# New homes for the split features and the contexts' matrices, input matrices on GpSimd's queue, and context rows that are turned without a trip to DRAM

## The chip, the cores and the metric

One of the eight cores of a Trainium2 chip runs the whole program. The metric is the device time of one execution in microseconds (us); a kernel's time is the median of several runs. A profile is one execution recorded by the chip's profiler, with instruction times counted from the start of its span.

## The reference

Two layers work on 512 latent tokens and 256 context tokens of width 1024, in float32. Each layer has a token mixer and a gated ConvFFN; layer 0 mixes by attention, layer 1 by a two-directional complex-diagonal state-space scan (S5). Each part is wrapped in RMSNorms with shift, scale and gate rows that come from conditioning vectors. Cut to what the change touches:

```
def conv_ffn(h, w_up, conv_w, conv_b, w_down):
    a = conv3(h @ w_up) + conv_b
    val, gate = split(a, 2)
    return (silu(gate) * val) @ w_down                       # D_FF = 2816

# end of layer 0, for latents and for contexts
x = x + m[5] * rms_norm(conv_ffn(h, ...), g_post_ffn[0])
# start of layer 1
h = modulate(rms_norm(x, g_pre_mix[1]), m[0], m[1])
# layer 1's mixer, for each of 2 directions
hc = s5_scan(u_c, lb, bb, None)          # contexts; u_c: 64 groups of 16 channels
hl = s5_scan(u_l, lb, bb, hc[end])       # latents start from the contexts' last state
y += s5_readout(hl, c)
o = (gelu(y + d*u) @ w_glu_a) * sigmoid(gelu(y + d*u) @ w_glu_b)
```

Contexts are needed in layer 1 only for the state in which they end.

## The kernel before

**Matmuls in three passes.** Float32 products are made of `fp32r` parts. Each weight block is split into a high and a low part, `whl` (ACT at L109, DVE at L110), and so are the features, `hs` (ACT at L942, DVE at L943). One product is then the three matmuls of L159, L160 and L161.

**The down projection of layer 0** (`ffn_down`, called twice from `ffn0`) goes over 22 blocks of 128 features. The first call makes three token tiles, the two of the contexts and the first of the latents; the second makes the latents' tiles 1 to 3. In each block, three tiles times two halves of the width times three passes are 18 matmuls of 128x512, named `dn`. The first three and the last four blocks are taken together, tile by tile (`together`), the others block by block. The call's `pool` (`self.hsp`) holds the split features `hs`, four slots in the first call and three in the second.

**The ends.** When a tile's product is complete, `done` calls `begin` and `end`. They multiply by the gate row (L741), take the statistics (ACT L740, and a row of tiny DVE instructions at L742 and L171 to L175), add the residual (L746), take statistics again (ACT L362) and modulate for layer 1 (L1035, L1036). Three gate, scale and shift rows, `rows`, are loaded broadcast to all partitions (L1010). The modulated tile `po` goes out by DMA: a context's to DRAM, `xnd` (L1038), a latent's into the SBUF tile `xc`, by blocks of 8 tokens (L1043). With the first call, the two contexts' and first latent tile's ends come between the two `ffn_down`; with the second call they are the last thing before the mixer.

**The contexts' part of layer 1** (`ssm_contexts`) is a generator. It loads `xcc` from `xnd` (L1571), reorders it (ACT L1425), transposes it on TensorE (`pu`, L1430) into `uc`, multiplies by the input matrices `Pt` (`pi`, L1494; eight groups of 512 KB pairs), turns the results back (`pb`, L1480; copied to `Bc` at L1485) and adds up states on DVE in two halves (`ssm_sums`, L1519 to L1522; `ssm_carry`, L1549 to L1552). `ffn_down` pulls steps of this generator between its blocks by `jobs=(24, 4, 15, jobs)` (24 steps spread over blocks 4 to 14), and its `before` pulls the rest ahead of the last four blocks.

**The latents' part** (`ssm`) begins with the loads of `lam` (L1555) and of further matrices, reorders `xc` into `xq` (L1425, on ACT and DVE), and transposes it (`pu`, L1430). `ssm_ahead` (L1396) makes a tile and a load for each matrix ahead of its use (L1411): `Pd` are the input matrices, `Qd` the output matrices. All of these loads go through SP's queue.

**What sets the order.** A tile scheduler orders each engine's queue from the order in which the program emits its instructions and from modelled costs. SBUF pools are stacks on a left and a right side; a tile placed on memory that another pool held waits for the last readers of what was there. In the kernel before, the second call's `hs` pool is made after `rowp` and lies on memory that the ends between the calls read.

Of the kernel before, what the change touches and what calls it, by code (L numbers as in the profile page):

```python
# [20 lines left out]
P = 128  # L21
# [13 lines left out]
G = 64  # L35
# [16 lines left out]
def dap(ap, off, dims):  # L52
    return bass.AP(tensor=ap.tensor, offset=ap.offset + off, ap=[list(d) for d in dims])
# [92 lines left out]
class Kernel:  # L146
# [831 lines left out]
    def ffn0(self):  # L978
# [28 lines left out]
        def rows_of(pool, lc):  # L1007
            t = pool.tile([P, 3, D], FT, name=f"rows{lc}")
            for i, (l, grp, m) in enumerate(((0, 2, 1), (1, 0, 0), (1, 0, 1))):
                nc.sync.dma_start(t[:, i], dap(self.mdram[l, grp], lc * 2048 + m * 1024, [[0, P], [1, D]]))  # L1010
            return [t[:, i] for i in range(3)]
# [7 lines left out]
        self.xnd = self.dram.tile([CTX, D], FT, name="xnd")  # L1019
# [7 lines left out]
        def end(wk, rows):  # L1027

            t, x = begun.pop(0)
            x, o = x()  # L1030
            if t >= NTC:
                nc.sync.dma_start(self.x2[t * P:(t + 1) * P, :], x)
            _, sh, gs = rows[int(t < NTC)]
            r = self.stats(x, wk.tile([P, D], BF, name="junk", tag="junk", bufs=1), "sx")
            v.tensor_tensor(o, x, gs, op=OP.mult)  # L1035
            self.mark = v.scalar_tensor_tensor(o, o, r, sh, op0=OP.mult, op1=OP.add).ins  # L1036
            if t < NTC:
                nc.sync.dma_start(self.xnd[t * P:(t + 1) * P, :], o)  # L1038
                return
            c, q = D // 2, nc.scalar if t == NT - 1 else nc.sync  # L1040
            for a in range(2):
                p0 = NCL * a + t - NTC
                q.dma_start(xc[p0:p0 + NCL - NT + NTC + 1:NT - NTC], o[:, a * c:(a + 1) * c])  # L1043
# [13 lines left out]
        rows = [rows_of(wk, i) for i in range(2)]  # L1057
# [38 lines left out]
        self.hsp.release()  # L1096
        rowp.release()
        si.release()
        self.hps[0].release()
# [296 lines left out]
    def ssm_ahead(self, loads, rooms, behind=None):  # L1396


        tiles = []
        rooms = [(pool, tag, bufs) for pool, tag, bufs in rooms for _ in range(bufs)]  # L1400
        for i in range(len(loads)):
            while len(tiles) < min(i + len(rooms), len(loads)):
# [8 lines left out]
                self.nc.sync.dma_start(t, src[:, gp:gp + n])  # L1411
                tiles.append(t)
            if i == 0:
                yield
# [144 lines left out]
    def ssm_contexts(self, si):  # L1559
# [7 lines left out]
        x = self.sb[1].tile([P, 2, 2048], FT, name="xcc", tag="B", bufs=1)  # L1567
        xcc = x[:, 0].rearrange("p (s c) -> p s c", s=TC)
        xq = x[:, 1].rearrange("p (g s c) -> p g s c", g=16, s=TC)
# [25 lines left out]
        for gp in self.ssm_inputs_turned(mats, lambda b: Bc[b // 2][:, b % 2], lambda g: uc[:, g % 16, g // 16], NCC, si):  # L1595
            if gp >= 12:
                next(first, None)
                next(first, None)
            yield
# [5 lines left out]
    def ssm(self):  # L1605
# [5 lines left out]
                              ((Rooms(None, Pt=[x[:, i] for x in hl for i in range(2)]), "Pt", 8), (sx, "Pt", 3)))  # L1611
# [12 lines left out]
        B = [x.tile([P, 2, NCL + 1, 2, 2, 8], FT, name="B", tag="B", bufs=1) for x in (self.sb[0], up)]  # L1624
        for i in range(2):
# [3 lines left out]
                            ((sp, "Qt", 8),), xq[0:1, 3, 7, 7, 15:16])  # L1629
# [279 lines left out]
```

## Time and profile before

| | |
|---|---|
| median of 3 runs | 1712.47 us (1712.05 to 1713.34) |
| the profiled execution | 1709.45 us |
| its span in the trace | 1707.7 us, 24431 instructions |
| TensorE busy (PE) | 1549.5 us, 91% |
| VectorE busy (DVE) | 1069.2 us, 63% |
| ScalarE busy (ACT) | 700.6 us, 41% |
| GpSimd busy (POOL) | 66.9 us, 4% |
| mean granted clock of TensorE | 0.958 of full speed |
| first `ffn_down`'s last matmul ends | 940.9 us |
| second `ffn_down`'s matmuls | 960.7 to 1072.9 us |
| the latents' first transpose | 1105.2 us |

Busy time is averaged over stages with different limits, so the shares say little by themselves; the stretch from 935 to 1110 us has to be read row by row. A row of the timeline gives start, duration, engine, line, operation and output from inputs; in brackets stands how long the engine was idle before it and what ended that wait. A queue's issues are marked with a "q" behind the engine's name.

### The profile page before, as it was taken

How to read it: one execution, taken by the hardware profiler on the slowest of the kernel's cores; microseconds unless marked ns; L12 is line 12 of the kernel's file. 1: busy time of each engine (PE TensorE's matmuls, PEld its weight loads, DVE VectorE, ACT ScalarE, POOL GpSimd, SP SyncE). 2: the span in 40 equal slices, each digit the busy share in tenths (PEclk: the TensorE clock that was granted, in tenths of full speed). 3: DMA queues.
4: the chain of work that ended last, by engine and by line, in shares of the span. 5: the costliest groups of instructions: out<-in, count | busy, mean ns of one | idle time of the engine just before them, and what ended most of it. 6: DMA issues, size and time to landing. Idle time of an engine off the chain costs nothing.

```text
span 1707.7 us, 24431 instructions
## 1 busy us (share of the span) xinstructions
PE 1549.5 (91%) x9300; PEld 1236.5 (72%) x9300; DVE 1069.2 (63%) x2185; ACT 700.6 (41%) x1379; POOL 66.9 (4%) x86
## 2 busy tenths in 40 slices
PE   5999789999999999989999599246999999999997
PEld 2775568888788887767888477234778887788886
DVE  4653687769777776777544636689535654545334
ACT  4465547756434333233343344241245443333322
POOL 0111230000000000000000000000011000000000
PEclk8999799999999999999999799677999999999999
DMA  9424450086445766686663665843544333432421
GB/s 311 133 74 144 170 186 26 30 271 226 144 142 159 204 165 194 141 239 145 221 247 139 191 232 171 266 152 93 155 134 133 94 106 116 126 110 100 159 74 50
DMA packets 223259, 263.44 MB, mean 154 GB/s; under 512 B 21038, under 2 KB 173526, under 8 KB 222502
## 3 DMA queue, kind: packets, MB, share of 16 engines
q1 hardware_dynamic: 222422, 261.28, 49.7%
q8 instruction: 73, 1.20, 0.3%
q10 hardware_dynamic: 336, 0.54, 0.1%
q14 instruction: 44, 0.36, 0.1%
q0 software_dynamic: 384, 0.07, 0.0%
HBM read 223.89 MB, written 35.85 MB: 152 GB/s over the span
## 4 chain that ended last, share of the span: by engine, by line
PE 79%; DVE 11%; DMA 4%; ACT 2%; SPq 1%; issue 1%; POOL 0%; DVEq 0%; ACTq 0%
PE up L159 11%; PE up L161 11%; PE up L160 11%; PE dn L159 6%; PE dn L160 6%; PE dn L161 6%; PE acc L159 2%; PE acc L161 2%; PE acc L160 2%; PE glu L161 2%; PE glu L159 2%; PE macc L301 2%; PE glu L160 2%; PE py L1703 1%; DMA wm<-in_w_mod 1%; PE wo L159 1%
## 5 line engine op out<-in xcount | busy, mean ns | idle before, releaser
L110 DVE TENSOR_TENSOR whl<-wraw,whl 128x1024 fp32r<-128x1024 f32 x206 | 250.8, 1223 | 170.4 <-ACT whl L109 168.7
L109 ACT ACTIVATE whl<-wraw 128x1024 fp32r<-128x1024 f32 x206 | 216.6, 1056 | 203.9 <-PE dn L161 100.3
L159 PE MATMUL up<-b,whl 128*128 128x256 f32 (+1 forms) x728 | 244.2, 339 | 5.1 <-ACT whl L109 4.5
L161 PE MATMUL up<-b,whl 128*128 128x256 f32 (+1 forms) x728 | 242.3, 334 | 0.2 <-DVE whl L110 0.2
L160 PE MATMUL up<-b,whl 128*128 128x256 f32 (+1 forms) x728 | 241.8, 334 | 0.1
L159 PE MATMUL dn<-whl,hs 128*128 128x512 f32 x440 | 173.1, 397 | 19.8 <-ACT hs L942 19.8
L160 PE MATMUL dn<-whl,hs 128*128 128x512 f32 x440 | 173.9, 397 | 0.0
L161 PE MATMUL dn<-whl,hs 128*128 128x512 f32 x440 | 171.9, 394 | 0.0
L159 PEld LDWEIGHTS up<-b,whl 128*128 128x128 f32 x728 | 136.7, 188 | 31.2 <-issue 9.6
L161 PEld LDWEIGHTS up<-b,whl 128*128 128x128 f32 x728 | 136.7, 188 | 17.8 <-issue 3.4
L160 PEld LDWEIGHTS up<-b,whl 128*128 128x128 f32 x728 | 137.3, 189 | 15.7 <-issue 1.8
L877 DVE SCALAR_TENSOR_TENSOR ga<-up,cw,ga 128x511 f32<-128x511 f32 (+1 forms) x132 | 87.0, 659 | 93.6 <-ACT ga L873 92.1
L160 PE MATMUL up<-c,whl 128*128 128x512 f32 (+1 forms) x384 | 142.3, 372 | 0.0
L159 PE MATMUL up<-c,whl 128*128 128x512 f32 (+1 forms) x384 | 141.7, 375 | 0.7 <-DVE c L352 0.7
L161 PE MATMUL up<-c,whl 128*128 128x512 f32 (+1 forms) x384 | 142.0, 372 | 0.0
L159 PEld LDWEIGHTS dn<-whl,hs 128*128 128x128 f32 x440 | 83.5, 190 | 40.8 <-ACT hs L942 20.3
L873 ACT ACTIVATE ga<-up,cw 128x512 f32<-128x512 f32 x66 | 46.6, 706 | 159.3 <-PE up L161 157.7
L877 DVE SCALAR_TENSOR_TENSOR h<-up,cw,h 128x511 f32<-128x511 f32 (+1 forms) x132 | 86.8, 658 | 34.8 <-ACT h L873 33.5
L160 PEld LDWEIGHTS dn<-whl,hs 128*128 128x128 f32 x440 | 83.4, 190 | 20.1 <-issue 2.5
L161 PEld LDWEIGHTS dn<-whl,hs 128*128 128x128 f32 x440 | 83.2, 189 | 18.2 <-issue 0.4
L159 PEld LDWEIGHTS up<-c,whl 128*128 128x128 f32 x384 | 71.9, 188 | 17.0 <-issue 4.1
L161 PEld LDWEIGHTS up<-c,whl 128*128 128x128 f32 x384 | 72.2, 188 | 13.4 <-issue 0.4
(354 smaller groups left out, 2833.5 us busy)
## 6 DMA issues: line engine op xcount, KB each, us to landing
wraw<-in_w_up SPq DMA_DIRECT2D x88, 512.0 KB
wraw<-in_w_mod SPq DMA_DIRECT2D x80, 512.0 KB
wraw<-in_w_down SPq DMA_DIRECT2D x66, 512.0 KB
Pt<-Pd SPq DMA_DIRECT2D x32, 512.0 KB
wraw<-in_w_o SPq DMA_DIRECT2D x24, 512.0 KB
Pt<-Qd SPq DMA_DIRECT2D x32, 384.0 KB
wm<-in_w_mod SPq DMA_DIRECT2D x16, 512.0 KB
Pd<-Pb SPq DMA_DIRECT2D x16, 512.0 KB
```

What stands on the lines that cost most here:

```text
L109: nc.scalar.activation(w[:, 0], r, AF.Copy)
L110: e.tensor_tensor(w[:, 1], r, w[:, 0], op=OP.subtract)
L159: nc.tensor.matmul(out, a[0], b[0], start=start, stop=False)
L160: nc.tensor.matmul(out, a[0], b[1], start=False, stop=False)
L161: nc.tensor.matmul(out, a[1], b[0], start=False, stop=stop)
L301: nc.tensor.matmul(acc[32 * q:32 * q + 32], self.cT[:, k, :], w[:, 256 * q:256 * q + 256], start=(k == 0), stop=(k == KD - 1))
L873: nc.scalar.activation(o, acc, AF.Identity, scale=c[:, 1:2], bias=c[:, 3:4])
L877: nc.vector.scalar_tensor_tensor(x, acc[:, a + s:b + s], c[:, tap:tap + 1], x, op0=OP.mult, op1=OP.add)
L1703: nc.tensor.matmul(y[hs, i], x, t[hs, 2 + 2 * ri + d], start=False, stop=ri + d == 2)
```

## The change

- The first call's ends are only recorded while it runs (`ended`). After the call its features' pool, a work pool and the contexts' features are released, the second call's pool `hsc` and a pool `si` for five `Pt` slots (three before) and `xcc` are made in their place, the first `Pd` loads are started, and then the recorded ends are emitted.
- The rows are tiles of their own. For the second call two of three lie in `hpx`, beside the residuals.
- A context's modulated tile goes straight into `xcc` in SBUF, by four DMAs; `xnd` and its loads go. `uc` lies beside the reordered tile.
- All 32 `Pd` loads are issued from GpSimd's queue. `Qd` stays on SP; its loads behind the first are held back to the first one's issue, which waits for the last reordering copy.
- In `ssm`, two tiles are made ahead of `lam` in their pool.

```diff
-            if t < NTC:
-                nc.sync.dma_start(self.xnd[t * P:(t + 1) * P, :], o)
-                return
-            c, q = D // 2, nc.scalar if t == NT - 1 else nc.sync
-            for a in range(2):
-                p0 = NCL * a + t - NTC
-                q.dma_start(xc[p0:p0 + NCL - NT + NTC + 1:NT - NTC], o[:, a * c:(a + 1) * c])
+            y, n, k, i, m = (xcc[0], NCC, 4, t, NTC) if t < NTC else (xc, NCL, 2, t - NTC, NT - NTC)
+            c, q = D // k, nc.scalar if t == NT - 1 else nc.sync
+            for a in range(k):
+                q.dma_start(y[n * a + i:n * a + i + n - m + 1:m], o[:, a * c:(a + 1) * c])
...
-        self.ffn_down(tiles, ((1, 0, CTX), (0, 0, P)), 4, done_of(wk, rows, tiles), ends=4,
+        ended, xcc = [], []
+        self.ffn_down(tiles, ((1, 0, CTX), (0, 0, P)), 4, lambda *x: ended.append(x), ends=4,
                       before=lambda: load(wk, tiles))
-        wk.release()
         self.hsp.release()
         self.wkD.release()
         self.hps[1].release()
+        self.hsp = self.pool("hsc")
+        si = self.pool("ssmi")
+        xcc.append(si.tile([P, TC, D // 4], FT, name="xcc"))
+        mats = self.ssm_ahead([(self.Pd, gp, 2) for gp in range(0, G // 2, 2)], ((si, "Pt", 5),), nc.gpsimd)
+        next(mats)
+        for x in ended:
+            done_of(wk, rows, tiles)(*x)
+        wk.release()
...
-        si = self.pool("ssmi")
         rowp = self.pool("rowp")
-        rows = [rows_of(rowp, 0), None]
-        self.hsp = self.pool("hsc")
+        rows = [None, None]
         self.W.fence = self.W.limit = self.glu0
-        jobs = self.ssm_contexts(si)
+        jobs = self.ssm_contexts(xcc[0], mats)
...
-            x = self.hps[0].tile([P, 3, D], FT, name="hpx", tag=f"h{LAT}0", bufs=1)
+            x = self.hps[0].tile([P, 5, D], FT, name="hpx", tag=f"h{LAT}0", bufs=1)
...
+            rows[0] = rows_of(0, [x[:, 3], x[:, 4], rowp.tile([P, D], FT, name="row")])
             self.mats = self.ssm_ahead([(self.Pd, gp, 2) for gp in range(0, 10, 2)],
-                                       ((self.wp, "raw", 5),))
+                                       ((self.wp, "raw", 5),), nc.gpsimd)
...
-    def ssm_ahead(self, loads, rooms, behind=None):
+    def ssm_ahead(self, loads, rooms, queue, behind=None):
...
-                self.nc.sync.dma_start(t, src[:, gp:gp + n])
+                x = queue.dma_start(t, src[:, gp:gp + n])
+                if behind is not None and not tiles:
+                    held.enter_context(self.tc.issue_after(x.ins))
...
-        mats = self.ssm_ahead([(self.Pd, gp, 2) for gp in range(0, G // 2, 2)], ((si, "Pt", 3),))
-        next(mats)
...
-        for a in range(4):
-            nc.sync.dma_start(xcc[NCC * a:NCC * a + NCC],
-                              dap(self.xnd, a * (D // 4), [[TC * D, NCC], [D, TC], [1, D // 4]]))
...
-        uc = si.tile([P, 16, 4, NCC], FT, name="uc")
...
-        for _ in self.ssm_turn(xcc, xq, uc, (nc.scalar,) * 4):
+        for _ in self.ssm_turn(xcc, xq, uc, (nc.scalar,) * 4, NTC):
...
         up = self.pool("ssmv")
+        B1 = up.tile([P, 2, NCL + 1, 2, 2, 8], FT, name="B", tag="B", bufs=1)
+        u = up.tile([P, G, NCL], FT, name="u")
         self.lam_tile(up.tile([P, 2048], FT, name="lam"))
         lamR, lamI = self.lam
-        u = up.tile([P, G, NCL], FT, name="u")
```

**ACT where the first call hands over to the second**, before. `hs` (L942) with 128x384 are the second call's split features, `whl` (L109) its split weights, and `junk` with `sp` or `sx` (L740, L362) the ends' statistics.

```order
L942 ACTIVATE hs<-h_4350 128x256
L942 ACTIVATE hs<-h_4348 128x128
L740 ACTIVATE junk,sp<-dn 128x512 x3
L109 ACTIVATE whl_9287<-wraw_8960 128x1024
...
L362 ACTIVATE junk,sx<-px 128x1024
L740 ACTIVATE junk,sp<-dn 128x512 x2
L362 ACTIVATE junk,sx<-px 128x1024 x2
L942 ACTIVATE hs<-h_4347 128x384 x3
```

And now:

```order
L942 ACTIVATE hs<-h_4350 128x256
L942 ACTIVATE hs<-h_4348 128x128
L942 ACTIVATE hs<-h_4347 128x384 x3
L740 ACTIVATE junk,sp<-dn 128x512 x3
L109 ACTIVATE whl_9292<-wraw_8963 128x1024
...
L362 ACTIVATE junk,sx<-px 128x1024
L740 ACTIVATE junk,sp<-dn 128x512 x2
L942 ACTIVATE hs<-h_4347 128x384
```

The second call's first three blocks of split features stand ahead of the ends' statistics instead of behind them; the fourth stands behind two of three tiles' statistics.

**TensorE at the contexts' last step**, now. `pb` (line 1480 before, 1485 now) turns the last results back; `dn` are the second call's matmuls.

```order
L161 MATMUL dn<-whl_10062,hs 128x512
L1485 MATMUL pb<-ident,pe 128x128 x4
L159 MATMUL dn<-whl_10065,hs 128x512
L160 MATMUL dn<-whl_10065,hs 128x512
```

Of the call's 396 `dn` matmuls, 378 stand ahead of this step and 18 behind; before, 341 stood ahead and 55 behind. The contexts' first `pu` stood behind 54 `dn` matmuls before, and stands behind 173 now.

**DVE at the second call's end**, before. `t` and `Bc` (L1519 to L1522) are the second half of the contexts' sums, `hpo<-dn` (L741) is the first instruction of a latent tile's end.

```order
L1521 TENSOR_TENSOR t<-Bc_9514,lamc 128x2x128
L1522 TENSOR_TENSOR Bc_9514<-Bc_9514,t 128x8x32
L1519 TENSOR_TENSOR t<-Bc_9514,lamc 128x128 x2
L741 TENSOR_TENSOR hpo<-dn,rows_9256 128x512
L1522 TENSOR_TENSOR Bc_9514<-Bc_9514,t 128x8x32
```

And now (the sums are at L1524 to L1527):

```order
L1526 TENSOR_TENSOR t<-Bc_9519,lamc 128x1024
L1527 TENSOR_TENSOR Bc_9519<-Bc_9519,t 128x32x32
L741 TENSOR_TENSOR hpo<-dn,hpx 128x512
L1524 TENSOR_TENSOR t<-Bc_9519,lamc 128x512 x2
L741 TENSOR_TENSOR hpo<-dn,hpx 128x512
L742 TENSOR_TENSOR sp<-sp 128x1
L1527 TENSOR_TENSOR Bc_9519<-Bc_9519,t 128x32x32
```

Two of the second half's instructions of sums stand ahead of the first end's instruction, where all but the last sum did before.

## Rows read from the trace of the kernel before

**Rows 1.** The page's chain that ended last: shares of the span by engine.

```profile
PE 79%; DVE 11%; DMA 4%; ACT 2%; SPq 1%; issue 1%; POOL 0%; DVEq 0%; ACTq 0%
```

**Rows 2.** Busy time by windows of 20 us (the columns are in its first row).

```profile
core 0: us, PE busy (x) PEld busy (x) DVE busy (x) ACT busy (x) POOL busy (x), PEclk, DMA share, GB/s
940.00:960.00 20.00, 0.88 (x4) 0.38 (x3) 19.68 (x55) 6.39 (x12) 0.00 (x0) 0.64 0.74 263
...
1080.00:1100.00 20.00, 0.00 (x0) 0.00 (x0) 14.27 (x45) 4.32 (x11) 0.00 (x0) 0.50 0.80 249
```

**Rows 3.** The timeline of PE around the handover from first to second call.

```profile
940.26 0.39 PE L160 MATMUL dn<-whl,hs 128*128 128x512 f32 x1
940.49 0.39 PE L161 MATMUL dn<-whl,hs 128*128 128x512 f32 x1
960.72 0.79 PE L159 MATMUL dn<-whl,hs 128*128 128x512 f32 x1 [19.84 <-ACT hs L942]
```

**Rows 4.** The timeline of ACT in the same stretch.

```profile
938.37 2.25 ACT L109 ACTIVATE whl<-wraw 128x1024 fp32r<-128x1024 f32 x2
940.92 1.06 ACT L109 ACTIVATE whl<-wraw 128x1024 fp32r<-128x1024 f32 x1 [0.30 <-PE dn L161]
...
960.14 1.35 ACT L942 ACTIVATE hs<-h 128x384 fp32r<-128x384 f32 x3 [4.24 <-DVE po L1036]
```

**Rows 5.** The timeline of PE, the latents' first transpose.

```profile
1105.17 2.15 PE L1430 MATMUL pu<-ident,xq 128*128 128x128 f32 x9 [32.29 <-DVE xq L1425]
```

**Rows 6.** The timeline of DVE before and behind the second gap.

```profile
1093.32 1.28 DVE L1036 SCALAR_TENSOR_TENSOR hpo<-hpo,rsx,rows 128x1024 f32<-128x1024 f32 x1
1104.60 1.43 DVE L1425 COPY xq<-xc 128x512 f32<-128x512 f32 x4 [9.99 <-DMA Pt<-Qd]
```

**Rows 7.** The timeline of ACT, contexts' last `Bc` and last store into `xc`.

```profile
1060.44 1.12 ACT L1485 ACTIVATE Bc<-pb 128x256 f32<-128x256 f32 x2 [2.83 <-PE pb L1480]
...
1094.64 1.26 ACTq L1043 DMA_DIRECT2D xc<-hpo  x2
```

**Rows 8.** The timeline of SP's queue, 930 to 1130 us.

```profile
960.14 1.24 SPq L1043 DMA_DIRECT2D xc<-po  x2
964.46 2.52 SPq L1571 DMA_DIRECT2D xcc<-xnd  x4
...
1030.43 48.17 SPq L1411 DMA_DIRECT2D Pt<-Pd  x21
...
1094.82 0.33 SPq L1555 DMA_DIRECT2D lam<-lamd  x1
1095.20 14.34 SPq L1411 DMA_DIRECT2D Pt<-Qd  x8
```

**Rows 9.** Windows of 2 us behind the handover (columns as in group 2).

```profile
964.00:966.00 2.00, 2.00 (x6) 1.52 (x5) 0.00 (x0) 0.00 (x0) 0.00 (x0) 0.50 0.06 15
966.00:968.00 2.00, 2.00 (x10) 1.64 (x9) 0.00 (x0) 0.00 (x0) 0.00 (x0) 0.97 1.05 237
```

**Rows 10.** The timeline of DVE, contexts' second half of sums.

```profile
1061.59 1.23 DVE L1521 TENSOR_TENSOR t<-Bc,lamc 128x1024 f32<-128x1024 f32 x1 [2.67 <-ACT Bc L1485]
...
1067.31 0.55 DVE L943 TENSOR_TENSOR hs<-h,hs 128x384 fp32r<-128x384 f32 x1
...
1071.82 0.69 DVE L741 TENSOR_TENSOR hpo<-dn,rows 128x512 f32<-128x512 f32 x1 [0.39 <-ACT junk L740]
1072.43 0.41 DVE L1522 TENSOR_TENSOR Bc<-Bc,t 128x256 f32<-128x256 f32 x1
```

**Rows 11.** GpSimd's instructions that issue DMAs: busy, mean ns of one, idle.

```profile
L313 POOL DMA_DIRECT2D md<-mbias x8 | 4.6, 570 | 715.1 <-DVE mbias L305 297.4 <-DVE mbias L309 178.8 <-DMA wraw<-in_w_mod 159.4
```

**Rows 12.** The view of the tile that those DMAs write.

```profile
DMA to landing us min/median/max: 2.0/3.8/6.0
```

**Rows 13.** PE's groups of lines, 960.7 to 1072.9 us.

```profile
L1494 PE MATMUL pi<-Pt,uc 128*32 128x256 f32 x128 | 12.0, 387 | 0.0
L1480 PE MATMUL pb<-ident,pe 128*128 128x128 f32 x32 | 4.9, 274 | 0.0
```

More of the change, by code (lines that the diff above doesn't have):

```diff
@@ L1005, in mods, with rows_of @@
                 yield from self.mods_ahead(ps, units, 2 - i)
[L1007 to L1011, printed above, removed]
+        def rows_of(lc, tiles):
+            for t, (l, grp, m) in zip(tiles, ((0, 2, 1), (1, 0, 0), (1, 0, 1))):
+                nc.sync.dma_start(t, dap(self.mdram[l, grp], lc * 2048 + m * 1024, [[0, P], [1, D]]))
+            return tiles
         self.ffn_up(0, ((self.act[0], LAT), (self.act[1], CTX)), "left", firsts,
@@ L1018, in ffn0 @@
         xc = sb0.tile([2 * NCL, TC, D // 2], FT, name="xc", tag="B", bufs=1)
-        self.xnd = self.dram.tile([CTX, D], FT, name="xnd")
         begun, loaded = [], {}
@@ L1056, in ffn0 @@
         wk = self.pool("wkE0", "right")
-        rows = [rows_of(wk, i) for i in range(2)]
+        rows = [rows_of(i, [wk.tile([P, D], FT, name=f"row{i}{j}") for j in range(3)]) for i in range(2)]
         tiles = (*range(NTC), NTC)
-        self.ffn_down(tiles, ((1, 0, CTX), (0, 0, P)), 4, done_of(wk, rows, tiles), ends=4,
+        ended, xcc = [], []
+        self.ffn_down(tiles, ((1, 0, CTX), (0, 0, P)), 4, lambda *x: ended.append(x), ends=4,
                       before=lambda: load(wk, tiles))
-        wk.release()
         self.hsp.release()
@@ L1095, in ffn0 @@
         self.ffn_down(tiles, ((0, P, LAT),), 3, done, jobs=(24, 4, 15, jobs), ends=4, before=before)
-        self.hsp.release()
         rowp.release()
         si.release()
+        self.hsp.release()
         self.hps[0].release()
@@ L1394, in lam_powers @@
         return lam
-    def ssm_ahead(self, loads, rooms, behind=None):
-        tiles = []
+    def ssm_ahead(self, loads, rooms, queue, behind=None):
+        tiles, held = [], ExitStack()
         rooms = [(pool, tag, bufs) for pool, tag, bufs in rooms for _ in range(bufs)]
@@ L1410, in ssm_ahead @@
                 t = t[:, :k].rearrange("p (a b n) -> p a b n", a=n, n=P)
-                self.nc.sync.dma_start(t, src[:, gp:gp + n])
+                x = queue.dma_start(t, src[:, gp:gp + n])
+                if behind is not None and not tiles:
+                    held.enter_context(self.tc.issue_after(x.ins))
                 tiles.append(t)
+            held.close()
             if i == 0:
@@ L1557, in lam_tile, with ssm_contexts @@
         self.lam = [lam[:, j] for j in range(2)]
-    def ssm_contexts(self, si):
+    def ssm_contexts(self, xcc, mats):
         nc, v, su = self.nc, self.nc.vector, self.su
         self.banks = (("aux", 2),)
-        mats = self.ssm_ahead([(self.Pd, gp, 2) for gp in range(0, G // 2, 2)], ((si, "Pt", 3),))
-        next(mats)
         lam = su.tile([P, 2, 4, 4, 2, 2, 8], FT, name="lamc")
         self.C0 = su.tile([P, 2, 2, 2, 2, 8], FT, name="C0")
-        x = self.sb[1].tile([P, 2, 2048], FT, name="xcc", tag="B", bufs=1)
-        xcc = x[:, 0].rearrange("p (s c) -> p s c", s=TC)
-        xq = x[:, 1].rearrange("p (g s c) -> p g s c", g=16, s=TC)
-        for a in range(4):
-            nc.sync.dma_start(xcc[NCC * a:NCC * a + NCC],
-                              dap(self.xnd, a * (D // 4), [[TC * D, NCC], [D, TC], [1, D // 4]]))
+        x = self.sb[1].tile([P, 2, 2048], FT, name="xqc", tag="B", bufs=1)
+        xq = x[:, 0].rearrange("p (g s c) -> p g s c", g=16, s=TC)
+        uc = x[:, 1].rearrange("p (g a j) -> p g a j", g=16, a=4)
         for i in range(4):
@@ L1594, in ssm_contexts @@
         first = half(0)
-        for gp in self.ssm_inputs_turned(mats, lambda b: Bc[b // 2][:, b % 2], lambda g: uc[:, g % 16, g // 16], NCC, si):
+        for gp in self.ssm_inputs_turned(mats, lambda b: Bc[b // 2][:, b % 2], lambda g: uc[:, g % 16, g // 16], NCC, sc):
             if gp >= 12:
@@ L1610, in ssm @@
         more = self.ssm_ahead([(self.Pd, gp, 2) for gp in range(10, G // 2, 2)],
-                              ((Rooms(None, Pt=[x[:, i] for x in hl for i in range(2)]), "Pt", 8), (sx, "Pt", 3)))
+                              ((Rooms(None, Pt=[x[:, i] for x in hl for i in range(2)]), "Pt", 8), (sx, "Pt", 3)), nc.gpsimd)
         next(more)
         up = self.pool("ssmv")
+        B1 = up.tile([P, 2, NCL + 1, 2, 2, 8], FT, name="B", tag="B", bufs=1)
+        u = up.tile([P, G, NCL], FT, name="u")
         self.lam_tile(up.tile([P, 2048], FT, name="lam"))
         lamR, lamI = self.lam
-        u = up.tile([P, G, NCL], FT, name="u")
         uv = u.rearrange("p (a g) j -> p g a j", a=2)
@@ L1623, in ssm @@
                 pass
-        B = [x.tile([P, 2, NCL + 1, 2, 2, 8], FT, name="B", tag="B", bufs=1) for x in (self.sb[0], up)]
+        B = [self.sb[0].tile([P, 2, NCL + 1, 2, 2, 8], FT, name="B", tag="B", bufs=1), B1]
         for i in range(2):
@@ L1628, in ssm @@
         qs = self.ssm_ahead([(self.Qd, gp, 1) for gp in range(G // 2)],
-                            ((sp, "Qt", 8),), xq[0:1, 3, 7, 7, 15:16])
+                            ((sp, "Qt", 8),), nc.sync, xq[0:1, 3, 7, 7, 15:16])
         next(qs)
```

## The prediction

> **What bounds the kernel now.** I read the page's chain first: three quarters and more of the span hang on TensorE [rows 1], so time is to be had where TensorE waits. The 20-us windows then show two holes, 940 to 960 us and 1080 to 1100 us, with 0.88 and 0.00 us of matmuls in 20; in both DVE is the busy engine, 19.68 and 14.27 us [rows 2].
>
> First hole: the first call's last matmul ends at 940.49 + 0.39 = 940.88, the second's first begins at 960.72 after 19.84 idle, ended by ACT's `hs` [rows 3]. On ACT that group of three splits had itself waited, 4.24 us, for DVE's L1036 [rows 4], the last instruction of the ends. The split reads features that were long there; what it waits for is memory that the ends still read. So the hole is a buffer's wait, while the weights for it were split at 938.37 to 941.98 [rows 4].
>
> Second hole: the last `dn` ends at T = 1105.17 - 32.29 = 1072.88 [rows 5]. DVE finishes the ends at 1093.32 + 1.28 = 1094.60, T + 21.7; then it is idle 9.99 us until its reordering copy at 1104.60 [rows 6]. The view blames a `Qd` load, but the copy reads `xc`, whose last stores ACT issued at 1094.64 [rows 7]. `lam` and eight `Qd` loads were issued on SP in those same microseconds, 1094.82 and 1095.20 on [rows 8].
>
> The profiled execution is 3.02 us under the median (1709.45 against 1712.47). I make the sum against the former and add 3.0.
>
> **The change, part by part.**
>
> *A. The first hole closes: -19.5.* The second call's three splits now stand on ACT ahead of the ends, in memory that only finished readers held. Three splits take 1.35 us [rows 4]. In the row before, weights for the first blocks are split by 941.98; one more block's can be late by part of a DVE subtraction, so I leave 0.3 us of 19.84. The later splits stand behind pieces of the ends. Block 3's `hs` stands behind two tiles' statistics; TensorE needs it only after 3 blocks of 18 matmuls at 0.23 us (spacing in [rows 3]), 12.3 us after 940.9, about when those statistics were done before. The ends' 19.7 us of DVE [rows 2] then lie beside matmuls.
>
> *B. No slow start: -2.1.* After the idle time, TensorE's granted clock is 0.50 (1.2 of 2.4 GHz): 6 matmuls in 2 us, against 10 once it is 0.97 [rows 9]. It stays low to 966, 5.3 us: some 15 matmuls in 5.5 us that take 3.4 at full clock. Without the hole there is no idle time for it to fall in.
>
> *C. Small stalls: +0.5.* DVE now shares its ends with the weights' subtractions of the next blocks. Bounds: 0 (all are early) and 5 us (four instructions of 1.28, as in [rows 6], ahead of a weight).
>
> A to C put the last `dn` at about 1051.8, 21.1 earlier.
>
> *D. The sums slip behind the end: +7.3.* The contexts' last `pb` had 55 `dn` behind it and has 18 now. Before, `Bc` was ready at 1060.44 + 1.12 = 1061.56 [rows 7], T - 11.3, and DVE added up from 1061.59 to 1072.43 + 0.41, with a 0.55 split, a 0.69 end instruction and 0.39 idle among it [rows 10]. So 9.2 us of sums lay before or beside the ends' start, of which only the last 0.4 came behind it. Now `pb` ends 18 x 0.227 = 4.1 us before T and `Bc` is ready 1.2 later [rows 7], T - 2.9. Ends begin at T - 1.06, as 1071.82 was [rows 10], so 1.84 us of sums fit ahead and 9.1 - 1.8 = 7.3 fall into a tail in which DVE has no room: it was busy to the end of it. Bounds: 0, if the ends' waits swallow them, and 9.1.
>
> *E. The last stores land sooner: -4.6.* From 1094.64 to the copies took 9.9 us, with `lam` (1 MB) and `Qd` loads issued beside them. Now `lam` no longer waits for the rows' last reader, and goes out some 3 us earlier, while `Qd` waits for the copies. The nearest row of such a store with little beside it: issued at 960.14, and the queue's next issue, which had to wait, at 964.46 [rows 8], 4.3 us. I take 5.3, since `lam` may still be moving; bounds 4.3 and 9.9. `Qd` itself is not due until output matrices are used, long behind the input products.
>
> *F. Loads through GpSimd: 0.* An issue there costs 0.57 us [rows 11]; 32 are 18 us of an engine that does nothing in this stretch [rows 2]. SP sheds `Pd` issues, 21 of which stretched over 48.17 us [rows 8], but no work behind them was late, so nothing is gained. Cover: five slots, two used per group; a group's period is 22 `dn` at 0.227, 1/8 of 12.0 and of 4.9 us [rows 13], 7.1 us, so a load has 2.5 periods, 17.8 us. GpSimd's loads landed in 2.0 to 6.0 us [rows 12], though these were small; SP's 384 KB loads follow each other at 14.34 / 8 = 1.8 us [rows 8]. Either end is well inside 17.8. The Trainium skill, "DMA: Bandwidth & Descriptors", section Issuing engine by pattern, gives simple loads to Sync's queue and calls that path generally faster, which speaks against this edit. By the same page's section Anatomy, a GpSimd DMA takes about 2.0 us plus its bytes at 436 KB per us, an estimate of 3.2 us for 512 KB: by that the sum stays where it is too, and only the rule's warning against the path stands against the rows' 0, as the third rival.
>
> *G. The contexts' direct route: 0.* Four small stores replace one to DRAM and a load back, and `xcc` is complete before TensorE asks for it: the first `pu` now stands behind 173 `dn`, 39 us after the handover. If it were late, `jobs` steps would wait in TensorE's queue with `dn` behind them; the ends finish about 961 [rows 4], 19 us before, so this cover is wide. The `pi` results, `pe`, move to another pool, which costs nothing unless its slot is waited for.
>
> Sum: -19.5 - 2.1 + 0.5 + 7.3 - 4.6 = -18.4. Profiled 1709.45 - 18.4 = 1691.0; median 1712.47 - 18.4 = 1694.1.
>
> **The rivals.**
>
> *R1: the hole is only half filled (1702).* The ends now compete with the splits on DVE, whose 19.7 us in the hole [rows 2] were without a pause. If a weight's subtraction stands behind an end's chain, TensorE waits there instead, and perhaps falls back to 1.2 GHz. For it: DVE is the only engine with no slack. Against: the first weights are split by 942 [rows 4]. At half of A and B, 10.8 is lost: 1694.1 + 10.8 = 1704.9; with a part of D absorbed (DVE and its backlog trail less behind an unhurried TensorE), about 1702.
>
> *R2: the tail does not grow (1687).* If the sums fill the ends' waits for statistics, D is 0: 1694.1 - 7.3 = 1686.8. Against: those waits were 0.4 us in all [rows 10].
>
> *R3: GpSimd's loads are late, and it gets slower (1723).* Between groups a load has 17.8 us. With a landing of L above that, the period is L / 2.5, and about six groups pay: at L = 25 it is 10.0, +17.4, which uses up the gain; at L = 30 it is 12.0, +29.4, 1723.5. TensorE would show it as waits of `pi` for `Pt`. The Trainium skill, "SBUF — State Buffer", section SBUF: two separate sides, tells how it could come about: DVE instructions of some kinds keep GpSimd from writing descriptors, and a DMA that took about 620 ns took 3100 beside them. Stretched so, fivefold, the rows' 6.0 us [rows 12] would be 30. Against: by the page that is float32 copies between SBUF tiles; here these are the four of L1425 at 1104.60 [rows 6], by when the loads are out, while GpSimd's issues beside DVE's other work took 0.57 on average [rows 11].
>
> *R4: the wait stays (1715).* If the new slots still lie on memory that the ends read, `hs` waits as before, A to C are nothing, and D and E remain: +2.7, 1715.2, within what can be told from no change. Against: the three splits moved ahead of the ends on ACT.
>
> **How the numbers follow.** Forecast 0.68, R1 0.14, R2 0.08, R3 0.06, R4 0.04. The forecast's own range: C 5 and E's 9.9 both at their bad ends give +9.1, D at 0 gives -7.3. The range for 8 in 10 goes from R2, 1687, to just over R1's 1702, 1702.5. It leaves out R3, R4 and the worse half of R1. About 0.2% (3.4 us) is what a measurement of this kernel can tell from no change: faster holds forecast, R1 and R2, 0.90; same R4, 0.04; slower R3, 0.06.
>
> **What the new profile would show.** A, B: TensorE's row `dn` behind the first call without an idle entry of more than 1 us, no window of clock 0.50 near 945 to 966. D: the last L1036 at 29 us behind the last `dn`, and sums among the ends. E: the copies about 5.3 us after the last store into `xc`. F: no wait of `pi` for `Pt`. The prediction is wrong if TensorE waits over 5 us between 941 and 1052, if the span from last `dn` to first `pu` of the latents is not about 35 us (32.3 before, plus D, less E), or if the part behind it changes by more than 3 us.

## The result, and the profile after

| | before | after |
|---|---|---|
| median | 1712.9 us (4 runs, 1712.05 to 1715.67) | 1691.91 us (1686.64 to 1693.25) |
| ratio | | 0.9864, interval 0.9836 to 0.9892 |
| profiled execution, span | 1709.45, 1707.7 | 1693.25, 1691.4 |

One run of the four, of 8518.77 us, was disturbed; it is in the median and left out of the range and the ratio. The forecast was 1694.1, in a range of 1687.0 to 1702.5; the gain is 21.0 us by the medians, where 18.4 was forecast.

To compare traces I cut them at moments that each one has: ACT's weight split that waits for the first call's last `dn` (940.92 before, 944.87 after), the second call's last `dn`, the last end, DVE's copies, and the latents' first `pu`. What lies ahead of the first cut wandered by 4 us between executions of the same kernel (940.69 in a second trace of the change), so spans can't be compared to a microsecond, but the stretches between cuts can: they came out within 0.4 us in both traces. "Cut to cut" below is the sum of the four stretches.

| stretch, us | before | after | second trace | forecast's change | measured change |
|---|---|---|---|---|---|
| first call's last `dn` to second call's last | 131.96 | 104.34 | 104.35 | -21.1 (A, B, C) | -27.6 |
| to the last end | 21.72 | 27.56 | 27.56 | +7.3 (D) | +5.8 |
| to DVE's copies | 10.00 | 9.32 | 9.71 | -4.6 (E) | -0.3 to -0.7 |
| to the first `pu` | 0.57 | 0.57 | 0.57 | 0 | 0 |
| sum | 164.25 | 141.79 | 142.19 | -18.4 | -22.1 to -22.5 |

From the first `pu` to the end of the span it was 602.5 us before and is 604.8 and 603.8 now, 1.3 to 2.3 us longer. That is why the medians show less than the stretches; with the runs below between 602.8 and 605.6 it is hardly more than this part's own wander.

Busy time of the change by windows of 20 us (columns in the first row), to stand beside [rows 2]:

```profile
core 0: us, PE busy (x) PEld busy (x) DVE busy (x) ACT busy (x) POOL busy (x), PEclk, DMA share, GB/s
940.00:960.00 20.00, 20.00 (x90) 16.57 (x89) 19.56 (x49) 12.55 (x22) 2.11 (x4) 1.00 0.67 235
960.00:980.00 20.00, 20.00 (x90) 16.57 (x89) 16.70 (x34) 8.58 (x13) 0.00 (x0) 1.00 0.82 271
...
1060.00:1080.00 20.00, 0.00 (x0) 0.00 (x0) 16.37 (x59) 5.08 (x11) 1.57 (x3) 0.50 0.67 214
```

The first hole is gone: TensorE is busy for 20.00 us of the window that had 0.88, at clock 1.00 in place of 0.64, with DVE as full as before. The second hole is there still. TensorE's waits between 935 and 1110 us of the change (us in total, times, longest):

```profile
PE pu L1435 <- DVE xq L1430: 37.4, 1, 37.4
PE pi L1460 <- issue: 2.9, 2, 2.1
```

TensorE's timeline at the second hole, which was 32.29 us in [rows 5]:

```profile
1048.83 0.39 PE L161 MATMUL dn<-whl,hs 128*128 128x512 f32 x1
1086.66 4.94 PE L1435 MATMUL pu<-ident,xq 128*128 128x128 f32 x24 [37.45 <-DVE xq L1430]
```

DVE's timeline there, for [rows 6, 10]:

```profile
1046.30 1.23 DVE L1526 TENSOR_TENSOR t<-Bc,lamc 128x1024 f32<-128x1024 f32 x1 [3.14 <-ACT Bc L1490]
...
1048.70 0.68 DVE L741 TENSOR_TENSOR hpo<-dn,hpx 128x512 f32<-128x512 f32 x1
...
1058.42 0.42 DVE L1527 TENSOR_TENSOR Bc<-Bc,t 128x256 f32<-128x256 f32 x1
...
1067.95 0.21 DVE L1557 TENSOR_TENSOR C<-cw 128x64 f32<-128x64 f32 x1
...
1075.49 1.28 DVE L1034 SCALAR_TENSOR_TENSOR hpo<-hpo,rsx,hpx 128x1024 f32<-128x1024 f32 x1
1086.09 1.43 DVE L1430 COPY xq<-xc 128x512 f32<-128x512 f32 x4 [9.31 <-DMA xc<-hpo]
```

The sums run from 1046.30 to 1058.84, so they now lie among and behind the first instructions of the ends (1048.70), and the last end is done at 1075.49 + 1.28 = 1076.77, 27.56 behind the last `dn` at 1049.21. Then DVE waits 9.31 us for `xc`, nearly as long as the 9.99 of before.

### The profile page after: what moved, and what is told of

Its sections match the earlier page's. It is cut to its first block, busy times and chain, and to the rows that moved or that the text cites. A ratio compares the mean times of both kernels' runs of the same rounds, so it can differ in the third digit from the quotient of the medians.

```text
span 1691.4 us, 24467 instructions
## 1 busy us (share of the span) xinstructions
PE 1549.9 (92%) x9300; PEld 1239.5 (73%) x9300; DVE 1066.6 (63%) x2185; ACT 700.4 (41%) x1379; POOL 83.9 (5%) x118
## 4 chain that ended last, share of the span: by engine, by line
PE 83%; DVE 9%; DMA 3%; ACT 2%; SPq 1%; issue 1%; ACTq 0%; POOL 0%; DVEq 0%
PE up L159 12%; PE up L161 12%; PE up L160 12%; PE dn L159 6%; PE dn L160 6%; PE dn L161 6%; PE acc L159 2%; PE acc L161 2%; PE acc L160 2%; PE macc L301 2%; PE glu L161 2%; PE glu L159 2%; PE glu L160 2%; PE py L1703 2%; DMA wm<-in_w_mod 1%; PE macc L241 1%
## 5 line engine op out<-in xcount | busy, mean ns | idle before, releaser
L109 ACT ACTIVATE whl<-wraw 128x1024 fp32r<-128x1024 f32 x206 | 216.7, 1056 | 199.9 <-PE dn L161 98.7
L160 PE MATMUL dn<-whl,hs 128*128 128x512 f32 x440 | 171.7, 392 | 0.0
L159 PE MATMUL dn<-whl,hs 128*128 128x512 f32 x440 | 171.1, 393 | 0.0
L161 PE MATMUL dn<-whl,hs 128*128 128x512 f32 x440 | 170.9, 392 | 0.0
```

The source lines that it names most:

```text
L109: nc.scalar.activation(w[:, 0], r, AF.Copy)
L159: nc.tensor.matmul(out, a[0], b[0], start=start, stop=False)
L160: nc.tensor.matmul(out, a[0], b[1], start=False, stop=False)
L161: nc.tensor.matmul(out, a[1], b[0], start=False, stop=stop)
```

## The experiments

### The change once more

No edit.

> The changed kernel once more, for its spread and a second trace. Stretches, from the first call's last dn to the second call's last dn: 104.4 us in the first trace of it; from there to the latents' first pu 37.5 us. Theory: both come out again within 1 us, and the differences ahead of 940 us and behind the first pu do not. Rival: the stretches themselves wander by several us, then no term can be read from one trace.

1689.69 us (1688.34 to 1691.54), ratio 0.9873 (0.9856 to 0.9889). The stretches are in the table above: 104.35 and 37.84 us, within 0.4 of the first trace, while the time ahead of them differed by 4.2 us. In the experiments below that leave the second call's matmuls as they are, the first stretch is 104.34 or 104.35 us again, so it can be read from one trace; the wait behind the last end is known to some 0.4 us.

### The place of the slots alone

```diff
 # the kernel before
         self.hps[1].release()
+        self.hsp = self.pool("hsc")
...
         rows = [rows_of(rowp, 0), None]
-        self.hsp = self.pool("hsc")
...
-        self.hsp.release()
         rowp.release()
         si.release()
+        self.hsp.release()
```

> The kernel before with nothing but the second call's hs pool moved to the freed memory (the ends are emitted inside the first call as before, the contexts still go through DRAM, Pd on SP, three Pt slots). Theory: the hole is a wait for memory alone, so it closes here too: idle of TensorE there under 1 us, the second call's last dn some 21 to 23 us earlier than 1072.9. The contexts' last pb stands behind all dn in this order, so the tail grows by 9 us or more; total about -11, 1701. Rival: emitting the ends later is what closes it; then TensorE still waits 15 to 20 us and the total stays within 3 us of 1712.5 or above it.

1691.21 us (1690.36 to 1696.73), ratio 0.9885 (0.9867 to 0.9904). TensorE has no wait at the handover, and the last `dn` ends 106.7 us behind the first call's: 25.3 earlier than before. So the hole was a wait for memory alone, and the ends need not be emitted later for it. I had expected about 1701, since the contexts' last `pb` stands behind all `dn` here. It does, and TensorE waits for matrices ahead of it (its waits between 930 and 1062 us):

```profile
PE pi L1494 <- DMA Pt<-Pd: 6.4, 3, 5.0
```

But the end comes only 28.9 us behind the last `dn` (1050.24 to 1079.13), and the copies 4.46 us behind that, not 9.3. SP's queue shows why:

```profile
1074.02 0.33 SPq L1555 DMA_DIRECT2D lam<-lamd  x1
1080.62 1.40 SPq L1411 DMA_DIRECT2D Pt<-Pd  x3
1082.11 6.47 SPq L1411 DMA_DIRECT2D Pt<-Qd  x8
```

The last three `Pd` loads were issued at 1080.62, behind the last stores into `xc` (ACT issued them at 1079.16); in the change they go out ahead of them. That is what term E had missed, and is tried below. By the stretches this kernel (140.6) is level with the change (141.8, 142.2): the rest of the change gained 2.3 us up to the last `dn` and 1.3 in the tail, and lost 4.9 to 5.3 behind the last end.

### The queue of the loads

```diff
-((si, "Pt", 5),), nc.gpsimd)
+((si, "Pt", 5),), nc.sync)
...
-((self.wp, "raw", 5),), nc.gpsimd)
+((self.wp, "raw", 5),), nc.sync)
...
-(sx, "Pt", 3)), nc.gpsimd)
+(sx, "Pt", 3)), nc.sync)
```

> The changed kernel with its Pd loads back on SP's queue. TensorE's order is the same. Theory (the queue is worth nothing): within 2 us of the change, 1690 to 1693. Rival 1 (SP's queue is the better one): 3 us or more faster. Rival 2 (Pd loads waiting for their slots hold up the weights' loads behind them on SP): TensorE waits for whl or for Pt in the second call, 3 us or more slower.

1688.79 us (1686.84 to 1692.04), ratio 0.9866 (0.9849 to 0.9883), beside 1689.69 on the same chip. The stretch is 141.1 us. The queue is worth nothing either way, as term F had it. The view of the tile `Pt` in the change, 930 to 1100 us, has how long GpSimd's 512 KB loads took:

```profile
L1413 POOL DMA_DIRECT2D Pt<-Pd x32: 530/530/573, 931.5 to 1069.3; - x32
...
DMA to landing us min/median/max: 3.7/5.6/11.1
```

0.53 us for an issue, and at most 11.1 us to landing, inside the 17.8 that I had given a load between groups; no `pi` waits for `Pt` in either trace. The Trainium skill, "DMA: Bandwidth & Descriptors", section Issuing engine by pattern, gives plain loads to Sync's queue and calls that path the generally faster one; with these loads ahead of their use, no difference can be measured here.

### Three slots instead of five

```diff
-((si, "Pt", 5),)
+((si, "Pt", 3),)
```

> The changed kernel with three Pt slots instead of five. TensorE's row of dn is then interrupted 22 times by pu, pi and pb instead of 11, and the last pb stands behind all dn instead of 18 ahead of the end. Theory (each interruption costs TensorE about 0.45 us): the stretch of the second call's matmuls grows from 104.4 by about 5 us, the tail by up to 4; 1698 to 1701. Rival (interruptions are free, and the 5.7 us that the second call's row became shorter by have another source): the stretch stays at 104.4 within 1.5 us, only the tail grows; 1693 to 1695.

1704.54 us (1702.0 to 1705.42), ratio 0.9954 (0.9939 to 0.9969): 15 us slower than the change on the same chip, more than either theory gave. In the trace the last `dn` ends 108.53 us behind the handover instead of 104.35. TensorE's groups of `pi` in the second call, of the change, to stand beside [rows 13]:

```profile
L1499 PE MATMUL pi<-Pt,xqc 128*32 128x256 f32 x128 | 8.4, 384 | 0.0
```

and with three slots:

```profile
L1499 PE MATMUL pi<-Pt,xqc 128*32 128x256 f32 x116 | 11.6, 387 | 0.0
```

With five slots 128 of these took 8.4 us, in eight unbroken groups of 16; before it was 12.0, and with three slots 11.6 for 116 of them. With three slots most groups are split into twelve and four, and the results' transposes stand apart: 22 interruptions of the `dn` row instead of 11. One group in the change:

```profile
1005.47 0.39 PE L159 MATMUL dn<-whl,hs 128*128 128x512 f32 x1
1005.79 1.07 PE L1499 MATMUL pi<-Pt,xqc 128*32 128x256 f32 x16
1006.79 0.66 PE L1485 MATMUL pb<-ident,pe 128*128 128x128 f32 x4
...
1007.52 0.39 PE L161 MATMUL dn<-whl,hs 128*128 128x512 f32 x1
```

and with three slots:

```profile
1010.56 0.39 PE L159 MATMUL dn<-whl,hs 128*128 128x512 f32 x1
1010.88 1.06 PE L1499 MATMUL pi<-Pt,xqc 128*32 128x256 f32 x12
...
1012.20 0.40 PE L161 MATMUL dn<-whl,hs 128*128 128x512 f32 x1
...
1013.84 0.39 PE L159 MATMUL dn<-whl,hs 128*128 128x512 f32 x1
1014.16 0.63 PE L1499 MATMUL pi<-Pt,xqc 128*32 128x256 f32 x4
...
1015.05 0.39 PE L161 MATMUL dn<-whl,hs 128*128 128x512 f32 x1
...
1016.89 0.40 PE L160 MATMUL dn<-whl,hs 128*128 128x512 f32 x1
1017.12 0.60 PE L1485 MATMUL pb<-ident,pe 128*128 128x128 f32 x4
...
1017.80 0.39 PE L159 MATMUL dn<-whl,hs 128*128 128x512 f32 x1
```

Between the `dn` starts shown lie two spacings of 0.227 us each time. What is over is 1.60 us in the change, and 1.19, 0.76 and 0.46, together 2.41, with three slots: 0.8 us for two interruptions more, 0.4 each, near the 0.45 expected. TensorE waited for nothing else in that stretch. The 4.2 us are even a little short of the whole price, since the last twelve `pi` and the last `pb` stand behind the last `dn` here. That is the other part: the last `pb` starts at 1055.45, 3.1 us behind the last `dn` (1052.35) instead of 4.7 ahead of it, so the sums start later still; the last end comes 33.8 us behind the last `dn`. Cut to cut it is 152.7 us, 10.5 to 10.9 longer. The rest of the 15 lies outside these stretches; the time ahead of the first cut differs by such amounts between traces of one kernel, but what made it here isn't shown.

### What stands ahead of the last stores

Two runs: the last three `Pd` loads held behind the copies, by the same means as `Qd`'s first; and the other `Qd` loads not held behind that first.

```diff
-for gp in range(10, G // 2, 2)], ((Rooms(...), "Pt", 8), (sx, "Pt", 3)), nc.gpsimd)
+for gp in range(10, 26, 2)], ((Rooms(...), "Pt", 8),), nc.gpsimd)
...
+        late = self.ssm_ahead([(self.Pd, gp, 2) for gp in range(26, G // 2, 2)], ((sx, "Pt", 3),), nc.gpsimd, xq[0:1, 3, 7, 7, 15:16])
+        next(late)
...
-self.ssm_inputs(chain(self.mats, more), ...)
+self.ssm_inputs(chain(self.mats, more, late), ...)
```

And the second:

```diff
-                if behind is not None and not tiles:
-                    held.enter_context(self.tc.issue_after(x.ins))
```

> The changed kernel with the last three Pd loads (1.5 MB, needed by the last three of 16 input products) held back behind the reordering copies, as the Qd loads are. In the change they go out at 1064 to 1068, just ahead of the stores into xc. Theory (the last stores into xc stand behind these bytes): from the last end to the copies 4.5 to 6 us instead of 9.3 to 9.7, total 4 us less, about 1686. Rival 1 (lam's 1 MB and the stores themselves make the time): still 8 us or more, 1690. Rival 2 (the held loads come late for the products): a wait of pi for Pt behind the latents' pu takes the gain back.

> The changed kernel with the eight Qd loads (3 MB) free to go out all at once behind the first, instead of being held for the copies. The first still waits for the copies. Theory (the hold is only there in case the order on SP lets the others out early): in SP's order they already stand behind the first, so nothing changes, within 2 us of the change. Rival: they come ahead of it or beside the stores into xc, and the copies wait 3 us or more longer.

With the loads held: 1688.73 us (1687.99 to 1689.96), ratio 0.9862 (0.9847 to 0.9876). DVE's copies:

```profile
1081.44 1.43 DVE L1430 COPY xq<-xc 128x512 f32<-128x512 f32 x4 [6.21 <-DMA xc<-hpo]
```

6.21 us of wait instead of 9.31 and 9.71, and 138.7 us cut to cut instead of 142: the 1.5 MB ahead of the stores cost 3.1 to 3.5 us there. By the times the run can't be told from the change (ratios 0.9864 and 0.9873). In the change GpSimd issued them here:

```profile
1068.28 1.57 POOL L1413 DMA_DIRECT2D Pt<-Pd  x3 [17.71 <-issue]
```

right behind the contexts' last carry (1067.95 + 0.21 above), whose memory they take over. From then on the 16 DMA engines are busy without a pause, a mean share of 1.01, nearly until the copies; `lam` was issued at 1074.55 in this window and the last stores at 1076.81 (columns as in the windows above):

```profile
1070.00:1084.00 14.00, 0.00 (x0) 0.00 (x0) 6.50 (x16) 1.41 (x3) 0.00 (x0) 0.50 1.01 319
```

With `Qd` not held: 1692.58 us, ratio 0.988 (0.9863 to 0.9897), too little to tell from the change by the times. But the theory that nothing changes fell in the trace: two `Qd` loads went out at 1076.20 and 1077.01, beside ACT's last stores (1075.87 and 1076.55), and the copies came 10.9 us behind the last end, 1.2 to 1.6 more than in the change (143.4 us cut to cut). So by this one trace the hold does something, though less than the 3 us of the rival.

### The second half of sums on GpSimd

```diff
-            yield from self.ssm_sums(sc, Bc[i], 2 * i, lam)
+            e = nc.gpsimd if i else nc.vector
+            yield from self.ssm_sums(sc, Bc[i], 2 * i, lam, e)
...
-                self.ssm_carry(su, i, o, x, Bc[i][:, :, s_ + 7], lam)
+                self.ssm_carry(su, i, o, x, Bc[i][:, :, s_ + 7], lam, e)
```

> The changed kernel with the contexts' second half of sums and carries on GpSimd instead of DVE. Theory (DVE's instructions add up in the tail): from the last dn to the last end 27.6 falls by the 7.5 us of sums that lay behind the first end and by 2.7 of carries, to 18 to 20; since GpSimd's three last Pd loads then stand behind its sums, the stores into xc may land sooner, too; total 7 to 13 us less, 1677 to 1683. Rival 1 (the tail is the ends' chain of statistics and waits, not DVE's work): it falls by less than 3 us. Rival 2 (GpSimd's reads slow DVE's beside them): DVE's 128x1024 instructions in the tail take over 1.5 us instead of 1.22 to 1.28, and little is gained.

> Sums on GpSimd and the three loads held back. Theory: if both terms are what they seem, the gap from the second call's last dn to the latents' first pu falls from 37.5 to about 18.5 + 5 = 24 to 26; total about 1678. Rival: with the sums on GpSimd the three loads already come behind the stores, then holding them adds nothing and this is within 2 us of the run without it.

1695.94 us (1692.85 to 1698.65), ratio 0.9908 (0.9892 to 0.9925); with the loads held too 1691.28, ratio 0.9877 (0.9862 to 0.9892). Here, on one chip, the hold is worth 4.7 us by the times, and DVE's copies come 5.31 us behind the last end instead of 10.39:

```profile
1084.75 1.43 DVE L1430 COPY xq<-xc 128x512 f32<-128x512 f32 x4 [5.31 <-DMA xc<-hpo]
```

That confirms what the loads ahead of the stores cost. The sums on GpSimd gain nothing: DVE has 12 us less to do, 9 of them in the tail, and yet the tail is 32.8 us in both runs instead of 27.6. DVE's timeline without the hold:

```profile
1045.10 2.79 DVE L742 TENSOR_TENSOR sp<-sp 128x1 f32<-128x1 f32 x1
1047.81 0.68 DVE L741 TENSOR_TENSOR hpo<-dn,hpx 128x512 f32<-128x512 f32 x1
1048.41 0.14 DVE L171 TENSOR_SCALAR rsp<-sp 128x1 f32<-128x1 f32 x1
...
1049.26 1.17 DVE L175 SCALAR_TENSOR_TENSOR rsp<-rsp 128x1 f32<-128x1 f32 x1
...
1050.96 1.87 DVE L742 TENSOR_TENSOR sp<-sp 128x1 f32<-128x1 f32 x1
...
1062.74 1.75 DVE L746 SCALAR_TENSOR_TENSOR hpx<-hpo,rsp,hpx 128x1024 f32<-128x1024 f32 x1
```

and GpSimd's:

```profile
1045.53 2.33 POOL L1527 TENSOR_TENSOR Bc<-Bc,t 128x1024 f32<-128x1024 f32 x1
1047.95 2.47 POOL L1524 TENSOR_TENSOR t<-Bc,lamc 128x512 f32<-128x512 f32 x2
...
1057.03 2.12 POOL L1527 TENSOR_TENSOR Bc<-Bc,t 128x512 f32<-128x512 f32 x1
```

An instruction of 128x1 that takes 0.15 us elsewhere took 2.79, and ended at 1047.89, as GpSimd's instruction of 1045.53 ended at 1047.86; its row starts 0.43 us ahead of that one's, so that it was held by it is read from the common end. L746 took 1.75 instead of 1.28, and GpSimd's 128x512 at 1057.03 2.12 where another of that size took 1.25. The chain of statistics is made of such tiny instructions, so it is hit again and again. This is the behaviour told by the Trainium skill, "SBUF — State Buffer", section SBUF: two separate sides: a GpSimd instruction that reads SBUF and a DVE instruction with two SBUF inputs exclude each other for their whole length. The trace agrees: L741, one of whose inputs is in PSUM, kept its 0.68 us, and L171 and L172, with one input in SBUF, kept 0.14 to 0.15. Measured against its own length, the shortest instruction paid most here. So the second rival held, and with it fell the 1678 expected of sums and hold together.

### The second half of sums behind the ends

```diff
         first = half(0)
...
+        yield "half"
         yield from half(1)
...
+        part = takewhile(lambda x: x is None, jobs)
...
-            for _ in jobs:
+            for _ in part:
                 pass
...
-jobs=(24, 4, 15, jobs), ends=4, before=before)
+jobs=(24, 4, 15, part), ends=4, before=before)
+        with tc.issue_after(self.mark):
+            for _ in jobs:
+                pass
```

Two more runs add the hold of the three loads, and then all reordering copies on ACT.

> The changed kernel with the contexts' second half of sums and carries held back behind the last end, so that DVE does them while the stores into xc move. Theory (in the tail each sum of DVE lies on the path, behind it there is a wait of 9.7 us with DVE idle): from the last dn to the last end 18 to 20 us instead of 27.6; the three Pd loads and lam then go out earlier or meet the stores as before; first pu of the latents 6 to 9 us earlier; the sums that don't fit in the wait (12 us of work against 9.7) delay DVE's copies behind it, so total 4 to 8 us less, 1682 to 1686. Rival (the ends alone make the tail, by their chain of statistics): the last end stays later than 24 us and the total within 2 us of the change.

> The same with the last three Pd loads held back as well. Theory: the two waits add, first pu 3 us earlier again, but DVE's idle time is then only 6 us and 6 us of sums fall behind the copies; total 0 to 3 us under the run without the hold. Rival: DVE is the bound behind the copies, so what the stores gain DVE loses; same within 1 us.

> The same again with all reordering copies on ACT, so that DVE's sums hold no copy up. Theory: the latents' first pu comes 0.5 us later for ACT's slower copies (0.62 against 0.42), the rest is the same; total within 2 us of the run before. Rival: the copies on DVE stood behind sums there, then this is 2 us or more faster.

1681.61 us (1678.83 to 1683.94), ratio 0.9817 (0.9801 to 0.9834): 8 us under the change. DVE's timeline:

```profile
1067.66 1.29 DVE L1034 SCALAR_TENSOR_TENSOR hpo<-hpo,rsx,hpx 128x1024 f32<-128x1024 f32 x1
1068.87 1.22 DVE L1530 TENSOR_TENSOR t<-Bc,lamc 128x1024 f32<-128x1024 f32 x1
...
1073.96 0.69 DVE L1530 TENSOR_TENSOR t<-Bc,lamc 128x512 f32<-128x512 f32 x1
1075.09 1.43 DVE L1434 COPY xq<-xc 128x512 f32<-128x512 f32 x4 [0.43 <-DMA xc<-hpo]
```

The last end comes 20.76 us behind the last `dn` instead of 27.56, DVE fills its wait for `xc` with sums and idles 0.43 us, and cut to cut it is 131.9 us, 10 less than the change: 6.8 in the tail, and 3.2 to 3.6 behind it, where the copies come 6.1 us behind the last end. So the sums lay on the path of the tail, as term D had it, and needn't have. The 10 us stay: from the first `pu` to the end of the span it is 604.7 us here, and was 603.8 and 604.8 in the change's two traces.

Holding the three loads adds nothing: 1682.09, ratio 0.982 (0.9802 to 0.9838), 131.5 us. The rival's reason for that, that DVE would lose it again, isn't what the trace shows; without a hold, those loads already went out behind the copies of 1075.09:

```profile
1086.76 1.56 POOL L1417 DMA_DIRECT2D Pt<-Pd  x3 [37.23 <-issue]
```

since the memory that they take over is in use until the carries, which now come behind the copies. All copies on ACT: 1681.59, ratio 0.9819 (0.9804 to 0.9833), 131.7 us, the same.

### Two edits alone

The place of the slots and the sums behind the ends, in the kernel before, with nothing else of the change.

> The kernel before with two edits only: the second call's slots on the freed memory (as in the run of that alone, 1691.2), and the contexts' second half of sums behind the last end. No other part of the change. Theory (these two are all that pays; GpSimd's queue, the five slots and the direct route for the contexts are worth nothing together on top): from last dn to first pu of the latents 33.9 falls by 6 to 8 us, total 1682 to 1686, within 4 us of the change with the sums held behind. Rival (with the contexts' products standing behind all dn, and their loads late there, more sums are left than the wait for the stores holds): 1687 or more.

1690.43 us (1684.24 to 1694.41), ratio 0.9874 (0.9846 to 0.9902). The theory fell, by its time and by the trace, 139.0 us cut to cut against 131.9; the rival held. TensorE's waits between 930 and 1070 us:

```profile
PE pi L1498 <- DMA Pt<-Pd: 7.1, 3, 6.5
PE pu L1434 <- ACT xcc L1429: 3.2, 1, 3.2
```

The contexts' products now lack what the other parts give: their loads wait for three slots (7.1 us for `Pt`), `xcc` comes late (3.2 us), the last `pb` starts 12 us behind the last `dn` (1065.14, 1053.19), and the copies 8.2 us behind the last end, with two `Qd` loads issued from 1072.23 ahead of ACT's last stores at 1073.91. So the rest of the change, the five slots, the contexts' early start and direct route and the hold of `Qd` among it, is worth some 7 us together once the tail is short enough for it to show. What each part brings isn't separated.

## Why the prediction was right, and where its terms were off

**The whole** was right, 1691.91 for 1694.1, for the reason given: a wait for memory at the handover. TensorE has no wait of 5 us between 941 and 1052, which speaks against R1, R3 and R4, and the tail did grow, against R2. The span from the last `dn` to the first `pu` is 37.4 and 37.8 us, for "about 35", and the part behind it changed by 1.3 and 2.3 us, under the 3 named.

**A and B: right.** No wait of TensorE is left there and its clock stays at 1.00; the run of that edit alone shows that the place of the slots did it. From `dn` start to `dn` start the wait was 960.72 - 940.49, less one spacing, 20.0 us. The slow start was 2.6 us and not the 2.1 that I had priced: I took some 15 matmuls for it, from windows that count a matmul on an edge twice; the row has 13 spacings up to 966.29, which took 5.57 us and take 2.95 at 0.227.

**C: wrong, in sign.** I added 0.5 for small stalls, between 0 and 5, and didn't think of a gain. There is one of 5.0 us: the second call's own row of matmuls became shorter. Of the order I had read only the place of the last `pb` step, not that the `pi` and `pb` steps came in 11 interruptions of the `dn` row where 22 had been. The row's ends before:

```profile
966.29 0.40 PE L159 MATMUL dn<-whl,hs 128*128 128x512 f32 x1
...
1072.49 0.39 PE L161 MATMUL dn<-whl,hs 128*128 128x512 f32 x1
```

and its start in the change:

```profile
944.67 0.39 PE L159 MATMUL dn<-whl,hs 128*128 128x512 f32 x1
```

From first to last start the same 396 `dn`, with the same `pi` and `pb` among them, took 111.8 us before and take 104.2 now (last start at 1048.83). The 7.6 us between are 2.6 of slow start and 5.0 for 11 interruptions, 0.45 each. With three slots and all else as in the change, the 11 come back and cost 4.2 us. So 20.0, 2.6 and 5.0 make up the 27.6.

**D: right, 5.8 for 7.3.** The sums began at T - 2.9, as I had worked out; the first end's instruction came at T - 0.5 instead of T - 1.06, which gave them half a microsecond more room. My 9.2 and 9.1 us of sums were loose: the rows give 11.25 - 0.55 - 0.69 - 0.39 = 9.6 in all, 0.4 of which came behind the ends' start before already, so the growth was 9.2 - 1.8 = 7.4. Of the 1.5 us that are missing from it a half is that room, and 1.0 I can't place. It would fit that the sums now alternate with instructions of the ends whose rows overlap theirs by 0.08 us (1048.70 + 0.68 and the next at 1049.31), where before one sum's row started 0.04 behind the other's end; no run shows it. That DVE's sums were the cause is shown by the run that puts them behind the ends: 20.76 us, under the 21.72 of before.

**E: wrong.** The step that failed is "with little beside it". I forecast 5.3 us from the last end to the copies; it was 9.3 and 9.7. I had asked what of `lam` and `Qd` would be out of the way, and not what would come in their place: three `Pd` loads, 1.5 MB, whose memory came free at 1068.28, 8.5 us ahead of the last stores (1076.81), and the DMA engines were busy without a pause from 1070 to 1084. With them held it is 6.2 us, with the sums on GpSimd as well 5.3 for 10.4, and where they came later by themselves 4.5 and 6.1.

**F: right.** GpSimd's queue is worth nothing, and its loads' landing, 3.7 to 11.1 us, is inside the cover; R3 had the gain used up at 25.

**G** wasn't tried alone. The last run shows that a late `xcc` costs 3.2 us in that setting; what the way through DRAM has in it isn't separated from the slots.

So the gain was put too low by 6.5 us in A to C and by 1.5 in D, and too high by some 4 in E. That the total came within 4 us by the stretches, and within 2.2 by the medians, is in part luck.

## What to carry to other kernels

A slot's wait that is a wait for memory costs one line to remove, once the profile shows an engine waiting for the last reader of something it has no use for; look there first, and then at what the freed time runs into. Where an engine bounds a tail, put work that isn't needed yet behind the tail, into the next wait, instead of on another engine whose instructions hold its own up, as GpSimd's did here. And ahead of a small store on which everything waits, ask which bytes will be in the queues at that moment: a load becomes due when its memory comes free, and that is often the same moment.

## What was not expected of the hardware

Each further interruption of a row of 512-column matmuls by the same few small ones cost 0.4 to 0.45 us of TensorE (5.0 us for 11 from before to after), so eight groups in one piece beat the same work in pieces. And a 128x1 instruction on DVE that takes 0.15 us elsewhere took up to 2.79 us beside one of GpSimd's 128x1024 additions.
